# A hybrid transformer on one core: value and gate blocks taken earlier, the norms' statistics placed with priority, and each boundary's third weight block prepared ahead of the tail

## The chip, the core and the metric

The kernel runs on one core of a Trainium2 chip: TensorE multiplies matrices into PSUM, VectorE, ScalarE and GpSimd work on rows of SBUF and PSUM, and SyncE's queue carries nearly all DMAs. The metric is the device time of one execution in microseconds; times are medians of several runs, and a profile is taken from one further execution.

## The reference, cut to what matters

Two layers over 512 tokens of width 1024, each a token mixer and a feed-forward, with RMS norms before and after:

```python
for layer in range(DEPTH):
    a = rmsnorm(h, ln_mix_pre[layer])
    mem_n = rmsnorm(mem, ln_mem[layer])              # 256 memory rows
    if layer < N_A_LAYERS:                           # layer A
        proj = a @ w_in_a[layer]                     # u, v (768 each), q_mem (256)
        main = chunked_spatial_gating(u, v, ...)     # gelu(u) * (w_s @ layernorm(gelu(v)) + b_s)
    else:                                            # layer B: 12 heads with a forget gate
        main = forgetting_attention(q, k_s, v_s, log_f_s)
    mixed = concat([main, memory_attention(q_mem, mem_n, w_mem_kv[layer])])
    h = h + rmsnorm(mixed @ w_out[layer], ln_mix_post[layer])
    f = rmsnorm(h, ln_ffn_pre[layer])
    f = (silu(f @ w_ffn_gate[layer]) * (f @ w_ffn_up[layer])) @ w_ffn_down[layer]
    h = h + rmsnorm(f, ln_ffn_post[layer])
```

All of it is float32.

## The kernel before

**Products in three matmuls.** A float32 operand is kept as two parts in a format that TensorE takes at full rate: a rounded copy (`hi`) and what is left (`lo`). ScalarE makes `hi` (a cast), VectorE `lo` (a subtraction; both in `split`, L241), and `mm3` (L193 to L195) multiplies hi by hi, hi by lo and lo by hi into one PSUM tile. Weights come by DMA into one of four `raw` tiles; `weight_parts` splits each half of 512 columns into a pair `whi`, `wlo` out of eight buffers each. The activations' parts (`act`) share a pool of 36 tiles.

**What sets the order.** The program is written in the order below; a scheduler then gives each engine its own list of instructions, which the engine runs strictly in that order, each waiting for what it reads. `tc.high_priority()` lets a scheduler place the instructions inside it sooner, `issue_after` later. PSUM tiles are taken by tags: `mm` and `lg` with three buffers each, `tr` with two.

**Norms.** `Norm` sums squares of the tokens (`add`). `finish` multiplies the sum on TensorE (`st`), VectorE adds the epsilon (`var`), GpSimd raises it to the power -1/2 (`r`, L262). `spread` spreads the result over all partitions by transposes on TensorE (`rb`), and VectorE copies it out.

**The start of layer A** (`layer_a`, from L568). While h's squares are summed, TensorE works on query and value projections. `value_block(j)` makes eight pieces for one third of the value columns, each piece 12 matmuls of 256 columns; three such blocks (24 pieces, v_1 to v_12 in the lists) are one filler queue. The start takes 1, 2, 1, 1 and 3 of them between its steps: the norm of h, the loads of the memory rows, the query's scaling, the sums of the memory rows, the memory keys' weights, the memory rows' norm (`norm.finish((0, NMEM))`, var_2 and rb_2). Then come the memory keys (ps_3, ps_4), the memory values (memv) and the memory attention of four heads, between whose steps the remaining 16 pieces are put, four to a head. After the attention `gate_inputs(m)` makes one gate block (u): 24 matmuls of 512 columns and a Gelu. `stats`, `normed` and `spatial` make the layer norm of the gated values (mv, rv, vhi, vlo) and the spatial product s; gate blocks 0, 1 and 2 stand between the attention and the first s.

**The boundaries** (`boundary`). At the end of the first mixer, of the first feed-forward and of the second mixer the same function closes one stage and opens the next. `tail(0)` to `tail(3)` are the last products of the old stage for four blocks of 128 tokens, each with its own norm (ss, v, r) and scaling of y; `turn` transposes y (yt), adds it to h, and makes the next stage's inputs (hs, xshi, xslo) and squares (sq) for half of the tokens. The next stage's first four weight blocks are multiplied with the first half of tokens in `group(..., lag=3)`: three blocks go in step, the fourth lags three inputs. The first two blocks' weights were prepared behind `tail(1)`, the third's and fourth's behind the last `turn` of the first half. The norm of that half (st_3, var_3, rb_3 at the first boundary) is finished inside the group.

Of the kernel before, what the change touches and what calls it, by code (L numbers as in the profile page):

```python
# [15 lines left out]
P = 128  # L16
T = 512
D = 1024
KT = 8
TB = T // P  # L20
NMEM = 256
# [5 lines left out]
RMS_EPS = 1e-6  # L27
# [13 lines left out]
def hybrid(ctx: ExitStack, tc: tile.TileContext, i: dict, out: bass.AP):  # L41
# [91 lines left out]
    def pair_of_parts(n=512, aside=False):  # L133
        if aside:
            return act("whi"), act("wlo")
        return (wp.tile([P, max(n, 512)], F32R, tag="hi", name=name("whi"), bufs=8)[:, :n],
                wp.tile([P, max(n, 512)], F32R, tag="lo", name=name("wlo"), bufs=8)[:, :n])
# [10 lines left out]

    def prepared(src, shape, eng=None):

        raw = wp.tile([P, 1024], F32, tag="raw", name=name("raw"), bufs=4)
        n = shape[0] * shape[1]
        dst = raw[:, :n].rearrange("p (a b) -> p a b", a=src.shape[1]) if len(src.shape) == 3 else raw[:, :n]
        last_load[0] = nc.sync.dma_start(dst, src)
        return weight_parts(raw, shape, eng)

    def weight_parts(raw, shape, eng=None):
        n = shape[0] * shape[1]
        parts = []
        for d in range(0, n, 512):  # L160
            pair = pair_of_parts(min(512, n - d))
            split(raw[:, d : min(d + 512, n)], *pair, eng)
            parts += cut(pair, shape[1])
        return parts
# [99 lines left out]
    class Norm:  # L264
# [16 lines left out]
        def finish(self, cols):  # L281

            c0, c1 = cols
            tbs = range(c0 // P, c1 // P)
            t0, t1 = c0 // P, c1 // P
            st = ps("tr", (P, 4), s="st")
            for tb in tbs:
                some = self.sums(tb, cols)
                for n, sq in enumerate(some):
                    PE.matmul(st[:, tb : tb + 1], sq, avg, start=n == 0, stop=n == len(some) - 1)  # L290
            v = small("var")
            V.tensor_scalar_add(v[:, t0:t1], st[:, t0:t1], RMS_EPS)
            rsqrt(self.r4[:, t0:t1], v[:, t0:t1], t1 - t0)

# [270 lines left out]
    def layer_a():  # L565
        a = parts("a")
# [27 lines left out]
        def value_block(j):  # L594

            w, o = [], []

            def load():
                for kh in range(2):
                    w.extend(prepared(i["w_a_v"][j, kh], (4, 256)))  # L600

            def piece(tk, kh):
                if kh == 0:
                    o.append(ps("mm", (P, 256), s="v"))
                c = slice(tk * P, (tk + 1) * P)
                for k in range(4 * kh, 4 * kh + 4):
                    mm3(o[tk], (a[k][0][:, c], a[k][1][:, c]), w[k], k == 0, k == KT - 1)
                if kh:
                    evacs.append(lambda: evacuate(tk))
                if pre.done:  # L610
                    while evacs:
                        evacs.pop(0)()

            def evacuate(tk):
                if tk % 2 == 0:
                    vg[j, tk // 2] = plain("vg", (P, 2, 256))
                A.activation(vg[j, tk // 2][:, tk % 2, :], o[tk], AF.Copy, scale=pre.r4[:, tk : tk + 1])

            return load, [lambda tk=tk, kh=kh: piece(tk, kh) for tk in range(TB) for kh in range(2)]

        with tc.tile_pool(name="sgu", bufs=1) as lp:
            bsp = lp.tile([P, NG, P], F32, name="bsp")
            fill = queue([value_block(j) for j in range(3)])
            outs = [ps(t) for t in ("mm", "lg")]
# [16 lines left out]
            memt = load_mem()  # L641
            pieces(1)
            pre.spread(FULL, rbc)
# [3 lines left out]
            norm = mem_sums(memt)  # L647
            pieces(1)
            xs = mem_inputs(0, memt)
            wk = mem_key_weights(0)  # L650
            norm.finish((0, NMEM))
            pieces(3)
            norm.spread((0, NMEM), rmem)
# [7 lines left out]
            with tc.issue_after(last_exp[0].ins):  # L661
                for vt in vg.values():
                    A.activation(vt, vt, AF.Gelu_apprx_tanh)
# [3 lines left out]
                   for n, x in enumerate(("ln_v_g", "ln_v_b"))])  # L667
# [5 lines left out]
                            compare_op=ALU.is_ge, fill=0.0, base=0, channel_multiplier=-1)  # L673
            us, vp = [], {}
            mv = lp.tile([P, TB, 2], F32, name="mv")
            rv = small("rv")

            wu = []

# [43 lines left out]

            gate_inputs(0)
            stats()
# [131 lines left out]
    def boundary(phase, post, pre, nnorm, dst, block, evac, scaled=None):  # L857
# [37 lines left out]
        with behind(phase_parts):  # L895
            ws = [block(n) for n in range(2)]
        tail(2)
        turn(0, range(2))
        tail(3, lambda: turn(0, (2,)))
        turn(0, (3,))  # L900
        ws += [block(n) for n in range(2, 4)]
        outs = group(ws, inputs(0), h0, ["mm", "lg"] * 2, lag=3,
# [139 lines left out]
    def feed_forward(layer, phase, xp, meanwhile=None):  # L1042
# [32 lines left out]

        def first(n):
            return prepared(i["w_up" if n % 2 else "w_gate"][layer, n // 2], (KT, P))

# [50 lines left out]
    def layer_b(phase, fp):  # L1129
# [16 lines left out]
        def evac_first(outs, cols):  # L1146
            for m, o in zip(first, outs):
                queries(m, o, cols)

        a, close = boundary(phase, G_FFN_POST, G_MIX_PRE + 1, bnorm, rbc,  # L1150
                            lambda n: prepared(i["w_b_q"][first[n]], (KT, P)), evac_first)
        for m in range(2, 6):
# [256 lines left out]
```

## Time and profile before

| what | value |
|---|---|
| median of 3 runs | 1122.04 us (1121.86 to 1122.38) |
| the profiled execution | 1121.42 us, of which the span of its instructions 1119.7 us |
| VectorE, ScalarE busy | 80%, 59% of the span |
| DMA | 118.12 MB in all, 105 GB/s on average |

The span runs from the first to the last instruction of the profile; the rest of the execution's time lies around it. A busy share is an average over stages. Where TensorE loses time is read from the waits of its matmuls and of its weight loader (PEld), which stand in the part on the prediction. Each row of a timeline gives start, duration, engine, line, operation, what it writes and reads, shape, how often in a row, and in brackets the engine's idle time before it with what ended it.

### The profile page before, as it was taken

How to read it: one execution, taken by the hardware profiler on the slowest of the kernel's cores; microseconds unless marked ns; L12 is line 12 of the kernel's file. 1: busy time of each engine (PE TensorE's matmuls, PEld its weight loads, DVE VectorE, ACT ScalarE, POOL GpSimd, SP SyncE). 2: the span in 40 equal slices, each digit the busy share in tenths (PEclk: the TensorE clock that was granted, in tenths of full speed). 3: DMA queues.
4: the chain of work that ended last, by engine and by line, in shares of the span. 5: the costliest groups of instructions: out<-in, count | busy, mean ns of one | idle time of the engine just before them, and what ended most of it. 6: DMA issues, size and time to landing. Idle time of an engine off the chain costs nothing.

```text
span 1119.7 us, 19536 instructions
## 1 busy us (share of the span) xinstructions
PE 1107.3 (99%) x7409; PEld 1002.7 (90%) x7409; DVE 892.0 (80%) x1721; ACT 660.3 (59%) x1388; POOL 28.5 (3%) x41
## 2 busy tenths in 40 slices
PE   8999999999999999999999999999999999999998
PEld 6998889999899899998988898889999899899996
DVE  7979448999598578796968889958998598588776
ACT  7775458755266255476757677768765266255453
POOL 0100001000000000001000000001000000000000
PEclk9999999999999999999999999999999999999999
DMA  7413231334224234244242655421235234233222
GB/s 265 151 49 109 77 97 58 100 108 151 76 89 140 74 99 127 76 135 148 63 128 59 153 128 137 135 76 57 65 106 152 74 101 133 70 109 118 76 76 76
DMA packets 63557, 118.12 MB, mean 105 GB/s; under 512 B 5164, under 2 KB 39992, under 8 KB 63464
## 3 DMA queue, kind: packets, MB, share of 16 engines
q1 hardware_dynamic: 62584, 116.05, 33.8%
q8 instruction: 58, 0.95, 0.4%
q0 software_dynamic: 192, 0.52, 0.2%
q10 hardware_dynamic: 688, 0.31, 0.1%
q14 instruction: 35, 0.29, 0.1%
HBM read 104.71 MB, written 2.10 MB: 95 GB/s over the span
## 4 chain that ended last, share of the span: by engine, by line
PE 86%; DVE 7%; ACT 3%; issue 2%; POOL 1%; DMA 1%; SPq 0%; POOLq 0%; DVEq 0%; ACTq 0%
PE y L193 9%; PE y L195 9%; PE y L194 9%; PE a L194 5%; PE a L193 5%; PE a L195 5%; PE ps L195 3%; PE ps L194 3%; PE ps L193 3%; PE e L193 3%; PE e L194 3%; PE x L194 3%; PE x L193 3%; PE x L195 3%; PE e L195 3%; DVE wlo L241 2%
## 5 line engine op out<-in xcount | busy, mean ns | idle before, releaser
L241 ACT CAST whi<-raw 128x512 fp32r<-128x512 f32 x460 | 276.2, 620 | 267.0 <-PE y L195 118.6
L241 DVE TENSOR_TENSOR wlo<-raw,whi 128x512 fp32r<-128x512 f32 x460 | 305.2, 685 | 108.8 <-ACT whi L241 106.6
L193 PE MATMUL y<-whi,fhi 128*128 128x512 f32 (+1 forms) x356 | 140.0, 394 | 0.0
L194 PE MATMUL y<-wlo,fhi 128*128 128x512 f32 (+1 forms) x356 | 139.4, 392 | 0.0
L195 PE MATMUL y<-whi,flo 128*128 128x512 f32 (+1 forms) x356 | 139.4, 392 | 0.0
L194 PE MATMUL a<-xslo,whi 128*128 128x256 f32 x320 | 90.0, 281 | 0.0
L194 PE MATMUL x<-xslo,whi 128*128 128x256 f32 x320 | 89.9, 281 | 0.0
L195 PE MATMUL x<-xshi,wlo 128*128 128x256 f32 x320 | 89.9, 281 | 0.0
L193 PE MATMUL x<-xshi,whi 128*128 128x256 f32 x320 | 89.8, 281 | 0.0
L193 PE MATMUL a<-xshi,whi 128*128 128x256 f32 x320 | 89.8, 281 | 0.0
L195 PE MATMUL a<-xshi,wlo 128*128 128x256 f32 x320 | 89.8, 281 | 0.0
L193 PEld LDWEIGHTS y<-whi,fhi 128*128 128x128 f32 x356 | 66.9, 188 | 15.7 <-ACT fhi L241 0.7
L195 PEld LDWEIGHTS y<-whi,flo 128*128 128x128 f32 x356 | 66.9, 188 | 15.5 <-DVE flo L241 0.2
L194 PEld LDWEIGHTS y<-wlo,fhi 128*128 128x128 f32 x356 | 67.0, 188 | 14.7 <-DVE wlo L241 0.2
L193 PE MATMUL ps<-xshi,whi 128*128 128x256 f32 (+1 forms) x224 | 67.5, 304 | 0.0
L195 PE MATMUL ps<-xshi,wlo 128*128 128x256 f32 (+1 forms) x224 | 67.1, 302 | 0.1
L194 PE MATMUL ps<-xslo,whi 128*128 128x256 f32 (+1 forms) x224 | 66.4, 299 | 0.0
L193 PEld LDWEIGHTS a<-xshi,whi 128*128 128x128 f32 x320 | 60.4, 189 | 0.4
L194 PEld LDWEIGHTS a<-xslo,whi 128*128 128x128 f32 x320 | 60.3, 188 | 0.3
L193 PEld LDWEIGHTS x<-xshi,whi 128*128 128x128 f32 x320 | 60.4, 189 | 0.0
L195 PEld LDWEIGHTS x<-xshi,wlo 128*128 128x128 f32 x320 | 60.3, 189 | 0.0
L194 PEld LDWEIGHTS x<-xslo,whi 128*128 128x128 f32 x320 | 60.3, 188 | 0.0
(283 smaller groups left out, 3091.1 us busy)
## 6 DMA issues: line engine op xcount, KB each, us to landing
raw<-in_w_gate SPq DMA_DIRECT2D x44, 512.0 KB, 3.6
raw<-in_w_up SPq DMA_DIRECT2D x44, 512.0 KB, 3.5
raw<-in_w_down SPq DMA_DIRECT2D x44, 512.0 KB, 4.0
raw<-in_w_out SPq DMA_DIRECT2D x16, 512.0 KB, 4.5
raw<-in_w_b_q SPq DMA_DIRECT2D x8, 512.0 KB, 3.5
raw<-in_w_a_v SPq DMA_DIRECT2D x6, 512.0 KB, 7.0
raw<-in_w_a_u SPq DMA_DIRECT2D x6, 512.0 KB
raw<-in_w_v SPq DMA_DIRECT2D x6, 512.0 KB, 3.7
```

What stands on the lines that cost most here:

```text
L193: PE.matmul(o, w[0], x[0], start=start, stop=False, skip_group_check=more)
L194: PE.matmul(o, w[0], x[1], start=False, stop=False, skip_group_check=more)
L195: return PE.matmul(o, w[1], x[0], start=False, stop=stop, skip_group_check=more)
L241: last_parts[:] = A.copy(hi, src), (eng or V).tensor_sub(lo, src, hi)
```

## The change

Four edits in one diff; no instruction is added or taken away on any engine, only places and tiles change.

1. The start of layer A takes 1, 2, 2, 2 and 5 value pieces instead of 1, 2, 1, 1 and 3. So the weights of the second value block are loaded and split ahead of the memory keys', and v_5 and v_6 come ahead of the memory keys. The memory rows' `finish` is written ahead of the memory keys' weights. The third value tile takes the PSUM tag `lg`.
2. Gate block 0 becomes four pieces at the end of the filler queue. With 12 value pieces spent at the start, 12 value pieces and these four fill the attention. Its Gelu follows those of the values.
3. In `Norm.finish`, var and the power stand under `tc.high_priority()`.
4. At each boundary the third block is prepared with the first two, behind `tail(1)`, and its parts lie in four tiles of the large pool instead of the pool of weight parts. Only the fourth is left for later.

```diff
-    def prepared(src, shape, eng=None):
+    def prepared(src, shape, aside=False):
...
-            pair = pair_of_parts(min(512, n - d))
-            split(raw[:, d : min(d + 512, n)], *pair, eng)
+            pair = pair_of_parts(min(512, n - d), aside)
+            split(raw[:, d : min(d + 512, n)], *pair)
...
             v = small("var")
-            V.tensor_scalar_add(v[:, t0:t1], st[:, t0:t1], RMS_EPS)
-            rsqrt(self.r4[:, t0:t1], v[:, t0:t1], t1 - t0)
+            with tc.high_priority():
+                V.tensor_scalar_add(v[:, t0:t1], st[:, t0:t1], RMS_EPS)
+                rsqrt(self.r4[:, t0:t1], v[:, t0:t1], t1 - t0)
...
-                    o.append(ps("mm", (P, 256), s="v"))
+                    o.append(ps("lg" if (j, tk) == (0, 2) else "mm", (P, 256), s="v"))
...
-            fill = queue([value_block(j) for j in range(3)])
+            us, wu = [], []
+
+            def gate_block(m):
+
+                o = []
+
+                def load():
+                    wu.append(prepared(i["w_a_u"][m], (KT, P)))
+
+                def piece(n):
+                    if n == 0:
+                        o.append(ps("mm", s="u"))
+                    for k in range(2 * n, 2 * n + 2):
+                        mm3(o[0], wu[m][k], a[k], k == 0, k == KT - 1)
+                    if n == 3:
+                        us.append(plain("u"))
+                        V.tensor_mul(us[m], o[0], rbc)
+
+                return load, [lambda n=n: piece(n) for n in range(4)]
+
+            fill = queue([value_block(j) for j in range(3)] + [gate_block(0)])
...
             memt = load_mem()
-            pieces(1)
+            pieces(2)
             pre.spread(FULL, rbc)
...
             norm = mem_sums(memt)
-            pieces(1)
+            pieces(2)
             xs = mem_inputs(0, memt)
+            norm.finish((0, NMEM))
             wk = mem_key_weights(0)
-            norm.finish((0, NMEM))
-            pieces(3)
+            pieces(5)
             norm.spread((0, NMEM), rmem)
...
-                for vt in vg.values():
+                for vt in (*vg.values(), us[0]):
                     A.activation(vt, vt, AF.Gelu_apprx_tanh)
...
-            gate_inputs(0)
             stats()
...
         with behind(phase_parts):
-            ws = [block(n) for n in range(2)]
+            ws = [block(n, n == 2) for n in range(3)]
         tail(2)
         turn(0, range(2))
         tail(3, lambda: turn(0, (2,)))
         turn(0, (3,))
-        ws += [block(n) for n in range(2, 4)]
+        ws.append(block(3, False))
```

**TensorE around rb_2**, the broadcast of the memory rows' norm. Before (ps_3 is the first memory key block, v_1 to v_12 are value tiles):

```order
L193 MATMUL ps_3_533<-mparts_4_393,whi_9_410 128x256
L194 MATMUL ps_3_533<-mparts_4_393,whi_9_410 128x256
L195 MATMUL ps_3_533<-mparts_4_393,wlo_9_411 128x256
L259 MATMUL rb_2_496<-ident_91,r4_2_359 128x128 x2
L193 MATMUL ps_3_533<-mparts_5_396,whi_10_414 128x256
L194 MATMUL ps_3_533<-mparts_5_396,whi_10_414 128x256
L195 MATMUL ps_3_533<-mparts_5_396,wlo_10_415 128x256
```

and with the change:

```order
L193 MATMUL v_6_523<-whi_12_400,ahi_8_132 128x256
L194 MATMUL v_6_523<-wlo_12_401,ahi_8_132 128x256
L195 MATMUL v_6_523<-whi_12_400,alo_8_133 128x256
L259 MATMUL rb_2_549<-ident_91,r4_2_372 128x128 x2
L193 MATMUL ps_3_586<-mparts_1_431,whi_13_465 128x256
L194 MATMUL ps_3_586<-mparts_1_431,whi_13_465 128x256
L195 MATMUL ps_3_586<-mparts_1_431,wlo_13_466 128x256
```

The broadcast stood in the middle of ps_3, 48 matmuls behind its sums; now it stands ahead of ps_3, behind v_5 and v_6 (24 matmuls each), 60 behind its sums. rb_1, of the norm of h, stood in front of v_3 and now stands in its middle, 12 matmuls later.

**VectorE at the same place**: the memory norm's var_2, the gain products of the memory rows (mparts) and the low parts of weights. Before:

```order
L246 SCALAR_TENSOR_TENSOR mparts_8_405<-mem_4_329,gains_89,mparts_8_405 128x256
L241 TENSOR_TENSOR wlo_9_411<-raw_5_408,whi_9_410 128x512
L241 TENSOR_TENSOR wlo_10_415<-raw_5_408,whi_10_414 128x512
L241 TENSOR_TENSOR wlo_11_421<-raw_6_418,whi_11_420 128x512
L241 TENSOR_TENSOR wlo_12_425<-raw_6_418,whi_12_424 128x512
L292 TENSOR_SCALAR var_2_433<-st_2_428 128x2
L241 TENSOR_TENSOR wlo_13_439<-raw_7_436,whi_13_438 128x512
```

and with the change:

```order
L246 SCALAR_TENSOR_TENSOR mparts_1_431<-mem_1_326,gains_89,mparts_1_431 128x256
L667 SCALAR_TENSOR_TENSOR q_1_368<-ps_1_181,rbc_115 128x512
L667 SCALAR_TENSOR_TENSOR q_2_369<-ps_2_182,rbc_115 128x512
L246 SCALAR_TENSOR_TENSOR mparts_2_434<-mem_1_326,gains_89,mparts_2_434 128x256
L293 TENSOR_SCALAR var_2_460<-st_2_455 128x2
L246 SCALAR_TENSOR_TENSOR mparts_3_437<-mem_2_327,gains_89,mparts_3_437 128x256
L246 SCALAR_TENSOR_TENSOR mparts_4_440<-mem_2_327,gains_89,mparts_4_440 128x256
```

var_2 stood behind all eight gain products and four low parts; now it stands behind the second gain product. The four low parts wlo_9 to wlo_12, now of the second value block, stand ahead of rb_1's copy.

**VectorE at the first boundary**: low parts of the third block (wlo_59, wlo_60) and the fourth (wlo_61, wlo_62). Before:

```order
L241 TENSOR_TENSOR xslo_3_1990<-hs_3_1986,xshi_3_1989 128x512
L826 SCALAR_TENSOR_TENSOR h_114<-yt_4_2016,gains_89,h_114 128x256
L241 TENSOR_TENSOR wlo_59_2037<-raw_29_2034,whi_59_2036 128x512
L826 SCALAR_TENSOR_TENSOR h_114<-yt_5_2106,gains_89,h_114 128x256 x2
L320 TENSOR_TENSOR sq_17_1944<-sq_17_1944,sq_22_2030 128x512
L241 TENSOR_TENSOR xslo_4_2027<-hs_4_2023,xshi_4_2026 128x512
L322 TENSOR_TENSOR sq_17_1944<-sq_17_1944 128x256
L241 TENSOR_TENSOR wlo_60_2041<-raw_29_2034,whi_60_2040 128x512
L241 TENSOR_TENSOR wlo_61_2047<-raw_30_2044,whi_61_2046 128x512
L241 TENSOR_TENSOR wlo_62_2051<-raw_30_2044,whi_62_2050 128x512
```

and with the change:

```order
L241 TENSOR_TENSOR xslo_3_2000<-hs_3_1996,xshi_3_1999 128x512
L844 SCALAR_TENSOR_TENSOR h_114<-yt_4_2026,gains_89,h_114 128x256
L241 TENSOR_TENSOR wlo_61_2047<-raw_30_2044,whi_61_2046 128x512
L321 TENSOR_TENSOR sq_17_1954<-sq_17_1954,sq_22_2040 128x512
L241 TENSOR_TENSOR xslo_4_2037<-hs_4_2033,xshi_4_2036 128x512
L323 TENSOR_TENSOR sq_17_1954<-sq_17_1954 128x256
L241 TENSOR_TENSOR wlo_62_2051<-raw_30_2044,whi_62_2050 128x512
L844 SCALAR_TENSOR_TENSOR h_114<-yt_5_2106,gains_89,h_114 128x256 x2
L844 SCALAR_TENSOR_TENSOR h_114<-yt_6_2122,gains_89,h_114 128x256 x2
L241 TENSOR_TENSOR wlo_63_2357<-raw_31_2354,whi_63_2356 128x512
L241 TENSOR_TENSOR wlo_64_2361<-raw_31_2354,whi_64_2360 128x512
```

wlo_59 and wlo_60 are gone from here (they stand ahead of tail(2)'s first sum), wlo_61 and wlo_62 have taken their places, and wlo_63 and wlo_64, of the next stage, stand here too, ahead of var_3. On TensorE, rb_3 with the change:

```order
L290 MATMUL st_3_2210<-avg_106,sq_17_1954 128x1 x2
L195 MATMUL ps_13_2057<-xshi_4_2036,wlo_62_2051 128x256
L193 MATMUL ps_14_2248<-xshi_5_2116,whi_55_1876 128x256
L194 MATMUL ps_14_2248<-xslo_5_2117,whi_55_1876 128x256
L195 MATMUL ps_14_2248<-xshi_5_2116,wlo_55_1877 128x256
L193 MATMUL ps_15_2249<-xshi_5_2116,whi_57_1886 128x256
L194 MATMUL ps_15_2249<-xslo_5_2117,whi_57_1886 128x256
L259 MATMUL rb_3_2228<-ident_91,r4_3_1757 128x128 x2
```

Before, 23 matmuls stood between the sums st_3 and rb_3; now six.

More of the change, by code (lines that the diff above doesn't have):

```diff
@@ L154, in prepared, with weight_parts @@
         last_load[0] = nc.sync.dma_start(dst, src)
-        return weight_parts(raw, shape, eng)
-    def weight_parts(raw, shape, eng=None):
+        return weight_parts(raw, shape, aside)
+    def weight_parts(raw, shape, aside=False):
         n = shape[0] * shape[1]
@@ L673, in layer_a @@
                             compare_op=ALU.is_ge, fill=0.0, base=0, channel_multiplier=-1)
-            us, vp = [], {}
+            vp = {}
             mv = lp.tile([P, TB, 2], F32, name="mv")
             rv = small("rv")
-            wu = []
             def gate_inputs(m):
@@ L1074, in feed_forward, with first @@
         fs = [(act("fhi"), act("flo")) for _ in range(2)]
-        def first(n):
-            return prepared(i["w_up" if n % 2 else "w_gate"][layer, n // 2], (KT, P))
+        def first(n, aside):
+            return prepared(i["w_up" if n % 2 else "w_gate"][layer, n // 2], (KT, P), aside)
         def evac_first(outs, cols):
@@ L1150, in layer_b @@
         a, close = boundary(phase, G_FFN_POST, G_MIX_PRE + 1, bnorm, rbc,
-                            lambda n: prepared(i["w_b_q"][first[n]], (KT, P)), evac_first)
+                            lambda n, aside: prepared(i["w_b_q"][first[n]], (KT, P), aside), evac_first)
         for m in range(2, 6):
```

## The prediction

> **What bounds the kernel now.** I read the page first: busy shares, the granted clock, the chain that ended last.
>
> ```profile
> PE 1107.3 (99%) x7409; PEld 1002.7 (90%) x7409; DVE 892.0 (80%) x1721; ACT 660.3 (59%) x1388; POOL 28.5 (3%) x41
> ...
> PEclk9999999999999999999999999999999999999999
> ...
> PE 86%; DVE 7%; ACT 3%; issue 2%; POOL 1%; DMA 1%; SPq 0%; POOLq 0%; DVEq 0%; ACTq 0%
> ```
> TensorE is busy for 99% of the span, its clock is granted in every slice, and it carries 86% of the chain. The change adds and removes no matmul: it only puts work in another order. So it can only touch what TensorE loses between matmuls, at most the 1% idle on the page (1119.7 - 1107.3 = 12.4 us, 1.1%), and in the stretches it reorders far less. Next I read TensorE's waits in those stretches: in the first layer's start (20 to 100 us), then at the first of the three stage boundaries (160 to 193 us), where the weight loader (PEld) shows them best.
>
> ```profile
> PEld rb L259 <- POOL r L262: 2.6, 2, 1.9
> PEld mo L485 <- ACT pT L241: 0.6, 1, 0.6
> PEld tr L456 <- PE v L195: 0.5, 1, 0.5
> ...
> PEld yt L821 <- ACT y L814: 0.7, 1, 0.7
> PEld rb L259 <- POOL r L262: 0.4, 1, 0.4
> PEld ps L193 <- ACT whi L241: 0.2, 1, 0.2
> ```
>
> Columns: waiter, what ended the wait, us in total, times, longest. The first three rows are the start: 2.6 + 0.6 + 0.5 = 3.7 us, of which the two broadcasts of a norm's root (rb) lose 2.6, one 1.9 and so the other 0.7. The last three are the first boundary, 1.3 us; the third boundary (752 to 780 us) answers with the same three rows to the digit, and the second with one row of 0.3:
>
> ```profile
> PEld ps L195 <- DVE wlo L241: 0.3, 1, 0.3
> ```
>
> All of it together is about 6.6 us, 0.6% of the time. That is the ceiling of the change; 0.2% (2.2 us) is about what a measurement of this kernel can tell from no change.
>
> **The start of layer_a: rb_1 and rb_2.**
>
> ```profile
> 26.24 0.28 PE L195 MATMUL v<-whi,alo 128*128 128x256 f32 x1
> 26.99 0.65 PE L259 MATMUL rb<-ident,r 128*128 128x128 f32 x4 [0.47 <-POOL r L262]
> ...
> 35.44 0.28 PE L195 MATMUL ps<-mparts,wlo 128*128 128x256 f32 x1
> ...
> 37.44 0.43 PE L259 MATMUL rb<-ident,r 128*128 128x128 f32 x2 [1.73 <-POOL r L262]
> ...
> 25.29 0.16 DVE L292 TENSOR_SCALAR var<-st 128x4 f32<-128x4 f32 x1 [1.57 <-PE st L290]
> ...
> 31.86 2.49 DVE L241 TENSOR_TENSOR wlo<-raw,whi 128x512 fp32r<-128x512 f32 x4
> 34.27 0.15 DVE L292 TENSOR_SCALAR var<-st 128x2 f32<-128x2 f32 x1
> 34.34 2.48 DVE L241 TENSOR_TENSOR wlo<-raw,whi 128x512 fp32r<-128x512 f32 x4
> ...
> 25.53 1.41 POOL L262 TENSOR_TENSOR r<-var,mhalf 128x4 f32<-128x4 f32 x1 [22.60 <-DVE var L292]
> 34.49 2.89 POOL L262 TENSOR_TENSOR r<-var,mhalf 128x2 f32<-128x2 f32 x1 [7.56 <-DVE var L292]
> ```
>
> Matmuls of 256 columns start about 0.118 us apart, so after 26.24 the next could start at 26.36, and rb_1 starts at 26.99: 0.63 lost. Likewise 37.44 - 35.56 = 1.88 at rb_2. Both wait for GpSimd's power.
>
> rb_1 gets 12 value matmuls put ahead of it (12 x 0.118 = 1.41), so it is due at 27.77. The power ended at 25.53 + 1.41 = 26.94; then nothing is lost. But behind its var VectorE's next work is no longer gain products but the low parts of the value weights now loaded first (wlo_9 to wlo_11), and beside four such low parts the power took 2.89: it would end at 28.42, 0.65 late. I take 0.2 lost, nearer to the 1.41 row, whose neighbours were also VectorE operations: 0.7 - 0.2 = **0.5 saved** (0 to 0.7).
>
> rb_2: its sums (st_2) now stand 60 matmuls ahead of it instead of 48, because v_5 and v_6 come before the memory keys, and its var stands at once behind mparts_2 instead of behind four low parts (2.49). Walking VectorE's new order with rb_1 at 28.0 (an estimate): rbc copied by about 30, two query products of 0.6 and two gain products of 0.4 by 32.5, var by 33. TensorE reaches rb_2 at about 28.0 + 0.4 + 84 x 0.118 = 38.3. Between them are 5.3 us, against 2.89 for the slowest power: no wait, **1.9 saved** (1.6 to 1.9).
>
> **A rule beside the 2.89.** That power started 0.15 us behind the first of four low parts that ran end to end to 36.82, and ended 0.57 after the last; alone it takes about as much as that 0.57:
>
> ```profile
> 160.84 0.56 POOL L262 TENSOR_TENSOR r<-v,mhalf 128x1 f32<-128x1 f32 x1 [4.98 <-DVE v L795]
> ```
>
> The Trainium skill, "SBUF — State Buffer", section "SBUF: two separate sides", says that VectorE and GpSimd share a pair of ports under an exclusive lock, taken by a VectorE operation with two SBUF inputs, and that "the other fully blocks". By that rule the power behind var_2 would have to sit out six gain products and four low parts, to about 38.0 + 0.56, and rb_2 would wait 0.3 instead of nothing. The power at 34.49 agrees; the one at 25.53, with three two-input operations behind its var, ended after 1.41, so the trace does not show it as strict. What a slow power would do at the other broadcasts is a rival below, priced from the rows.
>
> **The first transpose of the memory attention** (tr): four value pieces have moved from inside the attention to its front, and the softmax whose end it waits for still has 24 value matmuls between its last logits and the transpose; on VectorE, though, one of the value weights' low parts stands among its steps instead of three, so its products end 2 x 0.6 = 1.2 us earlier against the logits. I take its 0.5 as gone (0 to 0.5). The memory values (memv) come close instead: by the same walk their last low part is ready 0.4 us before its matmul. I book 0.1 lost (0 to 1.5, the delay of one slow power). The wait at mo (0.6) stays.
>
> **What pays for it: the gate block moved into the attention.** Before, three gate blocks stood between attention and the first spatial product; now two do.
>
> ```profile
> 89.10 0.15 DVE L694 TENSOR_SCALAR rv<-mv 128x4 f32<-128x4 f32 x1
> ...
> 94.45 0.68 DVE L241 TENSOR_TENSOR vlo<-vg,vhi 128x512 fp32r<-128x512 f32 x1
> ...
> 89.40 1.31 POOL L262 TENSOR_TENSOR rv<-rv,mhalf 128x4 f32<-128x4 f32 x1 [42.75 <-DVE rv L694]
> ...
> 97.16 0.40 PE L194 MATMUL ps<-alo,whi 128*128 128x512 f32 x1
> ...
> 98.56 0.40 PE L194 MATMUL ps<-alo,whi 128*128 128x512 f32 x1
> ...
> 100.90 0.27 PE L195 MATMUL s<-whi,vlo 128*128 128x128 f32 x1
> ```
>
> The second low part of the normed values is ready at 95.13, the first product that uses low parts starts at 100.90: 5.8 us of slack. A gate block is 24 matmuls of 512 columns, (98.56 - 97.16) / 6 = 0.233 apart: 5.6 us of that slack go. The chain gets shorter by what gate 0 had put in it on VectorE (two low parts and one product, 3 x 0.6 = 1.8) and longer by a seventh Gelu (0.6), so about 1.3 us of slack is left (an estimate). A power of 2.89 instead of 1.31 would use that up and 0.3 more. I book **0.1 lost** (0 to 1.6).
>
> Start together: -0.5 - 1.9 - 0.5 + 0.1 + 0.1 = **-2.7** (-3.1 with every lower price; +1.5 with every upper one).
>
> **The boundaries.** The third block's parts are cast and subtracted ahead of the last two token blocks' tail, while ScalarE and VectorE wait for TensorE there. So its 0.2 and the yt wait of 0.7 go, with some starts of 0.1 behind them: 12 matmuls of the third and 12 of the fourth block now stand ahead of the yt that waited. The yt groups shrink from five to two:
>
> ```profile
> 188.22 0.43 PE L259 MATMUL rb<-ident,r 128*128 128x128 f32 x2 [0.18 <-POOL r L262]
> 188.41 0.36 PE L195 MATMUL ps<-xshi,wlo 128*128 128x256 f32 x1
> 188.62 0.28 PE L193 MATMUL ps<-xshi,whi 128*128 128x256 f32 x1
> ```
>
> Behind a transpose the next step is 0.21 instead of 0.118; three groups fewer give about 0.2. But the fourth block now takes the third one's late places:
>
> ```profile
> 178.09 0.69 DVE L320 TENSOR_TENSOR sq<-sq,sq 128x512 f32<-128x512 f32 x1 [0.46 <-ACT sq L317]
> 178.70 0.69 DVE L241 TENSOR_TENSOR xslo<-hs,xshi 128x512 fp32r<-128x512 f32 x1
> 179.30 0.42 DVE L322 TENSOR_TENSOR sq<-sq 128x256 f32<-128x256 f32 x1
> 179.63 1.89 DVE L241 TENSOR_TENSOR wlo<-raw,whi 128x512 fp32r<-128x512 f32 x3
> ...
> 186.86 0.15 DVE L292 TENSOR_SCALAR var<-st 128x2 f32<-128x2 f32 x1
> ...
> 187.18 0.98 POOL L262 TENSOR_TENSOR r<-var,mhalf 128x2 f32<-128x2 f32 x1 [11.82 <-DVE var L292]
> ```
>
> wlo_62 stands behind the first three of these, the first of which waits for ScalarE's square of h as before; so it is done at 179.63 + 0.68 = 180.3. TensorE's first matmul here starts near 171.7; 48 of them at 0.118, eight transposes at 0.11 (with the 0.09 behind them) and eleven more matmuls later, at 179.6, it wants wlo_62: **0.7 lost**. From 180.3 on come thirteen matmuls, eight transposes and twenty-three matmuls (1.5 + 1.0 + 2.7): the sums st_3 at 185.5. rb_3 now stands six matmuls behind its sums instead of twenty-three (the fences on the change), so it is wanted at 186.4. Its var is behind two more low parts (wlo_63, wlo_64) but ahead of the last residual: by my walk at about 186.1; var to rb took 188.22 - 186.86 = 1.36; rb at about 187.5, so **1.1 lost** where 0.4 was. Two transposes and seven matmuls on (0.3 + 0.8) it stands at 188.6 where the kernel before stood at 188.62, the last row quoted for rb: **0.0** (-1.3 if wlo_62 is in time and rb_3 waits 0.5 as before; +1.9 if its power takes 2.89 instead of 0.98). The third boundary has the same rows and the same order: **0.0**. The second has four query blocks and 0.3 to save, and its var has less beside it: **-0.3** (-0.5 to 0.2).
>
> **Sum.** -2.7 + 0.0 + 0.0 - 0.3 = **-3.0 us**. The profiled execution took 1121.42 (span 1119.7), so 1118.4 in its frame; the median of the runs shown, 1122.04, is 0.6 above it, so I predict **1119.0**.
>
> **Rivals.** One more row bears on them, the power behind the second boundary, beside two low parts:
>
> ```profile
> 555.54 1.08 POOL L262 TENSOR_TENSOR r<-var,mhalf 128x2 f32<-128x2 f32 x1 [5.38 <-DVE var L292]
> ```
>
> - *The boundaries give all they hold.* If var_3 runs as soon as its sums are there and wlo_62 is in time, each saves 1.3: -2.7 - 2.6 - 0.3 = -5.6, **1116.4**. For it: the priority on var; against it: VectorE's order, in which wlo_62 stays behind a square it must wait for. 0.15.
> - *The cover was needed.* rb_1's 0.6, 0.5 at memv and 1.0 at the first spatial product eat the gain: -3.0 + 0.4 + 0.4 + 0.9 = -1.3, **1120.7**. For it: TensorE's slack there falls from 5.8 to about 1.3 us on my walk; against: each has slack, if little. 0.22.
> - *Slower: the power beside VectorE's stream.* If each power that now has low parts or sums behind its var takes 2.89, as at 34.49: 0.45 more at rb_1, 0.2 at the spatial product and 1.9 at each of the three boundaries. -3.0 + 6.35 = +3.35, **1125.4**. The place that decides is rb_3 and its two sisters: with everything else as forecast, the kernel is slower by 0.2% once their power passes 0.98 + (2.2 + 3.0) / 3 = 2.7 us. Against it: behind var_3 comes first a residual product out of PSUM, and beside two low parts the power took only the 1.08 of the row above. 0.06.
> - *It does nothing*: the waits reappear one step later, **1122.0**. The order shows the moved rows, so 0.05.
>
> **How the numbers follow.** The forecast has 0.52; most of its own spread (1118 to 1120.5) is under 1119.8, which is 0.2% below 1122.04; I give 0.44 of it to faster. Faster: 0.44 + 0.15 + 0.03 of the second = 0.62. Same: 0.08 + 0.19 + 0.05 = 0.32. Slower: 0.06. The range reaches from the first rival to just past the second, 1116.4 to 1121.4, and leaves out the slow power and part of no effect.
>
> **What would show it.** In the changed profile: rb at about 28 with under 0.3 of idle, rb at about 38 with none; memv (about 46) and the first spatial product (about 98) without a wait above 0.3; at 170 to 190 no wait at yt, but one at ps for wlo (0.7) and one at rb of about 1.0. It would be wrong if the rb waits at the boundaries pass 1.5 each, or if the spatial product waits over a microsecond.

## The result and the profile after

The changed kernel took **1114.91 us** (median of 5 runs, 1114.41 to 1117.99), the kernel before beside it 1121.88: 6.97 us less, a ratio of 0.9942 [0.9929, 0.9956]. The forecast was 1119.0 with a range of 1116.4 to 1121.4, so the sign was right, and the gain was more than twice the one forecast and outside the range. The profiled execution took 1114.41 (span 1112.7). The page's row of busy times:

```profile
PE 1103.1 (99%) x7409; PEld 1000.2 (90%) x7409; DVE 891.2 (80%) x1721; ACT 660.5 (59%) x1388; POOL 25.4 (2%) x41
```

TensorE's idle time went from 12.4 to 9.6 us (1112.7 - 1103.1): 2.8 us, close to the 3.0 forecast. But its *busy* time fell too, by 4.2 us (1107.3 - 1103.1), with the same 7409 matmuls. No step of the prediction had that. (The split is rough: the profile counts part of a short wait as busy, as at rb_1 before, where 0.63 us were lost and 0.47 show as idle.)

To find both I cut TensorE's list of matmuls at the same ones in every trace and took the time from start to start. All differences are to the first execution of the kernel before; the columns are explained with the experiments below. A "spot" is a short place inside a feed-forward that moves from execution to execution.

| stretch (us of the trace before) | before | before, again | changed | changed, again | start only | aside only | four aside | sums' own bank |
|---|---|---|---|---|---|---|---|---|
| first 100 matmuls, 1.3 to 24.3 | 23.04 | +0.52 | -0.55 | +0.22 | -0.03 | +0.58 | -0.13 | +0.32 |
| layer A, to 132.3 | 108.00 | -0.01 | **-3.51** | -3.48 | -3.47 | -0.01 | -3.53 | -3.52 |
| first boundary, to 211.3 | 79.00 | +0.01 | **-0.03** | -0.04 | -0.03 | -0.24 | +0.04 | -0.85 |
| second boundary, 516.8 to 564.5 | 47.66 | -0.01 | +0.02 | +0.03 | +0.15 | +0.03 | +0.01 | -0.35 |
| third boundary, 745.7 to 789.7 | 44.00 | -0.01 | +0.05 | +0.08 | +0.04 | +0.28 | +0.11 | -0.28 |
| first feed-forward, without 263 to 278 | 290.46 | 0.00 | **-1.28** | -1.27 | -1.01 | -0.45 | -0.77 | -1.04 |
| layer B, 564.5 to 745.7 | 181.18 | +0.01 | +0.01 | -0.02 | +0.07 | +0.07 | -0.11 | -0.01 |
| second feed-forward, without 851 to 865 | 251.54 | +0.05 | **-0.91** | -0.90 | -0.03 | -1.15 | +0.11 | -0.95 |
| end, from 1055.3 | 60.18 | +0.03 | -0.17 | -0.15 | +0.02 | -0.17 | +0.02 | -0.17 |
| spot at 263.4 to 278.5 | 15.09 | +1.02 | -0.77 | -0.15 | +0.15 | +0.19 | -0.70 | +0.18 |
| spot at 850.7 to 864.8 | 14.09 | +0.49 | -0.04 | +0.19 | +0.80 | -0.17 | -0.13 | +0.92 |

The -7.17 us of the first pair are: layer A -3.5, the boundaries nothing, the steady stretches of the feed-forward layers and the end -2.35, and the start's first matmuls and the two spots -1.35.

**The start.** These are TensorE's waits in the changed kernel as the weight loader shows them: the first two rows from 20 to 100 us, the next three from 155 to 190 (and the same three, to the digit, from 745 to 775), the last from 520 to 550.

```profile
PEld mo L486 <- ACT pT L241: 0.5, 1, 0.5
PEld vcols L749 <- PE ps L194: 0.4, 1, 0.4
...
PEld ps L195 <- DVE wlo L241: 0.8, 1, 0.8
PEld rb L259 <- POOL r L262: 0.5, 1, 0.5
PEld st L290 <- issue: 0.3, 1, 0.3
...
PEld st L290 <- issue: 0.3, 1, 0.3
```

The two waits at rb and the one at tr are gone from the start. The timeline around the two broadcasts and the first spatial product (start, duration, engine, line, operation, and the wait in front of it, if any):

```profile
27.11 0.28 PE L195 MATMUL v<-whi,alo 128*128 128x256 f32 x1
27.23 0.60 PE L259 MATMUL rb<-ident,r 128*128 128x128 f32 x4
...
38.33 0.28 PE L195 MATMUL v<-whi,alo 128*128 128x256 f32 x1
38.45 0.38 PE L259 MATMUL rb<-ident,r 128*128 128x128 f32 x2
...
96.88 0.27 PE L195 MATMUL s<-whi,vlo 128*128 128x128 f32 x1
...
24.98 1.41 POOL L262 TENSOR_TENSOR r<-var,mhalf 128x4 f32<-128x4 f32 x1 [22.05 <-DVE var L293]
31.71 0.90 POOL L262 TENSOR_TENSOR r<-var,mhalf 128x2 f32<-128x2 f32 x1 [5.32 <-DVE var L293]
...
25.42 1.89 DVE L241 TENSOR_TENSOR wlo<-raw,whi 128x512 fp32r<-128x512 f32 x3
...
31.56 2.46 DVE L246 SCALAR_TENSOR_TENSOR mparts<-mem,gains,mparts 128x256 fp32r<-128x256 f32 x6
...
95.14 0.68 DVE L241 TENSOR_TENSOR vlo<-vg,vhi 128x512 fp32r<-128x512 f32 x1
```

Each rb starts 0.12 behind the matmul ahead of it, one matmul's pace: no time is lost. rb_1's power was done at 24.98 + 1.41 = 26.39, 0.8 ahead of its broadcast, beside the three low parts that start at 25.42; rb_2's was done at 32.61, 5.8 ahead. The normed values' second low part was ready at 95.82 and wanted at 96.88: 1.06 us of slack, where 1.3 was worked out.

**The first boundary.** The same view at the places where the prediction walked:

```profile
175.54 0.69 DVE L241 TENSOR_TENSOR wlo<-raw,whi 128x512 fp32r<-128x512 f32 x1
...
181.17 0.87 DVE L844 SCALAR_TENSOR_TENSOR h<-yt,gains,h 128x256 f32<-128x256 f32 x2
182.41 0.16 DVE L293 TENSOR_SCALAR var<-st 128x2 f32<-128x2 f32 x1 [0.37 <-PE st L290]
...
181.38 0.27 PE L194 MATMUL ps<-xslo,whi 128*128 128x256 f32 x1
181.80 0.58 PE L290 MATMUL st<-avg,sq 128*128 128x1 f32 x4
...
182.91 0.28 PE L194 MATMUL ps<-xslo,whi 128*128 128x256 f32 x1
183.50 0.43 PE L259 MATMUL rb<-ident,r 128*128 128x128 f32 x2 [0.31 <-POOL r L262]
...
182.74 0.70 POOL L262 TENSOR_TENSOR r<-var,mhalf 128x2 f32<-128x2 f32 x1 [11.47 <-ACT sq L318]
```

This execution stands 0.55 + 3.51 = 4.06 ahead of the one before here. Put back by that, wlo_62 was done at 180.29 (forecast 180.3) and rb_3 stood at 187.56 (forecast 187.5). The new waits were 0.8 for wlo_62 (0.7 was priced), 0.3 in front of the sums and 0.5 in front of the broadcast (1.1 was priced, all of it at the broadcast), and they took the place of the old ones. var ran 0.37 us behind VectorE's work before it, as soon as its sums were there. The two low parts that stand ahead of it in VectorE's list, wlo_63 and wlo_64, had run long before and held nothing up:

```profile
177.71 1.28 DVE L241 TENSOR_TENSOR wlo<-raw,whi 128x512 fp32r<-128x512 f32 x2
```

### The profile page after: what moved, and what is told of

It is laid out like the page before. It is cut to its first block, busy times and chain, and to the rows that moved or that the text cites. A ratio compares the mean times of both kernels' runs of the same rounds, so it can differ in the third digit from the quotient of the medians.

```text
span 1112.7 us, 19537 instructions
## 1 busy us (share of the span) xinstructions
PE 1103.1 (99%) x7409; PEld 1000.2 (90%) x7409; DVE 891.2 (80%) x1721; ACT 660.5 (59%) x1388; POOL 25.4 (2%) x41
## 4 chain that ended last, share of the span: by engine, by line
PE 89%; DVE 5%; ACT 3%; issue 1%; DMA 1%; POOL 0%; SPq 0%; POOLq 0%; DVEq 0%; ACTq 0%
PE y L193 9%; PE y L195 9%; PE y L194 9%; PE a L195 5%; PE a L193 5%; PE a L194 5%; PE e L193 3%; PE e L195 3%; PE x L193 3%; PE x L195 3%; PE e L194 3%; PE x L194 3%; PE ps L195 3%; PE ps L193 3%; PE ps L194 3%; PE v L193 2%
```

## The experiments

**What varies by itself, and what belongs to the program.** Both kernels were run once more, unchanged. First the kernel before:

> The kernel before, unchanged, as a control. The two traces differ by 7.0 us of span: about 3.5 us lie at the start of layer A, 0.8 in one product at 266 us, 0.6 in the first hundred matmuls, which are the same in both, and some 2.2 us are spread thinly over stretches in which the order is the same (23.70 us for 200 matmuls of 256 columns before, 23.52 with the change). Theory 1, the thin part belongs to the execution: this run's 200 matmuls take anything from 23.5 to 23.7 and its time differs from the shared runs of before by up to 2 us. Theory 2, it belongs to the program: 23.70 again, within 0.03, and a ratio of 1.000 within 0.0005.

It took 1121.88 beside 1121.44, ratio 1.0004 [0.9995, 1.0012]. Its profiled execution was the longest of the set, 2.1 us above the first trace of before, and the table says where: in the first 100 matmuls and the two spots; all other stretches agree within 0.05. At the first spot ScalarE's casts wait for a weight that arrives by DMA. Before:

```profile
269.95 0.62 ACT L241 CAST whi<-raw 128x512 fp32r<-128x512 f32 x1 [1.32 <-DMA raw<-in_w_down]
```

and before, again, in the timeline and in TensorE's waits from 262 to 276:

```profile
271.94 1.14 ACT L241 CAST whi<-raw 128x512 fp32r<-128x512 f32 x2 [2.89 <-DMA raw<-in_w_down]
```

```profile
PE y L193 <- DVE s L1009: 0.8, 1, 0.8
PE e L193 <- ACT s L1003: 0.3, 1, 0.3
```

The cast waited 1.6 longer for the same load, and what stands behind it on ScalarE and VectorE made TensorE wait 0.8 where before it didn't. So this place is luck of an execution. The first 100 matmuls and the second spot also move between two executions of one program, by 0.2 to 0.8 us; what moves them was not followed up. The long stretch, by contrast, repeats. In the timelines of the kernel before, its first and last matmul are

```profile
278.47 0.39 PE L193 MATMUL y<-whi,fhi 128*128 128x512 f32 x1
...
516.85 0.39 PE L193 MATMUL y<-whi,fhi 128*128 128x512 f32 x1
```

and in its second execution

```profile
280.00 0.39 PE L193 MATMUL y<-whi,fhi 128*128 128x512 f32 x1
...
518.38 0.39 PE L193 MATMUL y<-whi,fhi 128*128 128x512 f32 x1
```

238.38 us both times for 1650 matmuls. In the changed kernel:

```profile
273.45 0.39 PE L193 MATMUL y<-whi,fhi 128*128 128x512 f32 x1
...
510.70 0.39 PE L193 MATMUL y<-whi,fhi 128*128 128x512 f32 x1
```

237.25. The busy times by stretch (columns: window, its length, then busy time and count of PE, PEld, DVE, ACT and POOL, the granted clock, the DMA share and GB/s) say that it is not a wait. Before, then changed:

```profile
278.50:516.80 238.30, 238.30 (x1651) 221.49 (x1650) 187.32 (x320) 121.82 (x242) 2.27 (x4) 1.00 0.35 107
```

```profile
273.40:510.70 237.30, 237.30 (x1651) 220.44 (x1651) 186.34 (x319) 121.61 (x242) 2.27 (x4) 1.00 0.36 107
```

TensorE is busy in every instant of both, with as many matmuls, at a granted clock of 1.00. Busy alone does not rule out short waits, since a matmul of 512 columns is booked for 0.39 us and the next starts 0.23 behind it. The gaps from start to start do: none of the 1650 is over 133 ns (256 columns) or 241 ns (512 columns) before, or over 125 and 244 ns in the changed kernel. So no single wait makes the difference; it is the same work at another pace. The changed kernel once more:

> The changed kernel, unchanged, as the other half of the control. Theory 1 (the thin part belongs to the execution): 200 matmuls anywhere from 23.5 to 23.7, ratio 0.994 to 0.997. Theory 2 (it belongs to the program): 23.52 within 0.03 and 0.9940 to 0.9945.

1116.08, ratio 0.9953 [0.9941, 0.9965]; its long stretches stand within 0.03 of the first changed execution's (237.26 for the one above); its spots do not. Without the three places the change is worth 7.17 - 1.35 = 5.8 us in the traces, and the medians of the two sets, 6.97 and 5.36, lie on both sides of that.

**Which part gives what.** The start alone, without the priority and with the boundaries as before:

```diff
-            with tc.high_priority():
-                V.tensor_scalar_add(v[:, t0:t1], st[:, t0:t1], RMS_EPS)
-                rsqrt(self.r4[:, t0:t1], v[:, t0:t1], t1 - t0)
+            V.tensor_scalar_add(v[:, t0:t1], st[:, t0:t1], RMS_EPS)
+            rsqrt(self.r4[:, t0:t1], v[:, t0:t1], t1 - t0)
...
-            ws = [block(n, n == 2) for n in range(3)]
+            ws = [block(n, False) for n in range(2)]
...
-        ws.append(block(3, False))
+        ws += [block(n, False) for n in range(2, 4)]
```

> The start of layer A and the moved gate block alone; no priority on the statistics, third block as before. If the start is worth what the trace shows there (3.5 us) and nothing else follows from it: 1118.3 to 1118.6, ratio 0.9970. If the thin part hangs on this half of the change: about 1116. Without the priority var_2 may stand behind the gain products again, and rb_2 wait up to 1 us: then 1119.5.

1118.09, 0.9972 [0.9962, 0.9983]. Layer A gives its 3.47 without the priority. And the first feed-forward gives 1.01, though from layer A's end on the lists of all five engines are those of the kernel before, instruction by instruction: only the tiles lie elsewhere, since layer A took them in another order.

The other half, the third block's parts in the large pool and nothing else:

```diff
-            ws = [block(n) for n in range(2)]
+            ws = [block(n, n == 2) for n in range(3)]
...
-        ws += [block(n) for n in range(2, 4)]
+        ws.append(block(3, False))
```

> The third block's parts prepared ahead of the tail, alone; start and statistics as before. Forecast theory (the removed waits return at the fourth block and at rb): 1121.5 to 1122.1. If rb keeps its late place because there is no priority: up to 1.3 us less at each of two boundaries, 1119.3. If the thin part or the product at 266 us hangs on this half: another 0.8 to 3 us less.

1119.99, 0.9985 [0.9977, 0.9994]. The three boundaries together give +0.06, nothing. What it gains is in the steady stretches: -0.45 and -1.15. Neither half has the priority on the statistics. The start saves as much without it as with it, and the first boundary came out at -0.24 without it and -0.03 with it, so no gain from the priority shows anywhere; it was not tried alone.

The start without its gate block, which stands behind the attention again:

```diff
-            fill = queue([value_block(j) for j in range(3)] + [gate_block(0)])
+            fill = queue([value_block(j) for j in range(3)])
...
-                for vt in (*vg.values(), us[0]):
+                for vt in vg.values():
...
+            gate_inputs(0)
             stats()
```

> The value pieces taken earlier and the memory norm's earlier place, without the gate block in the attention: the last head of the memory attention then has no filler between its steps. If the gate block is what pays for the earlier pieces, the waits of that head come out: a head has four pieces of 1.4 us, and its softmax chain is about as long, so 2 to 5 us back, 1120 to 1123. If it is not needed, the same 3.5 us are saved as with it (about 1118.1).

1118.42, 0.9972 [0.9961, 0.9983]. Layer A still gives 3.13. So the gate block is no cover that the rest needs; it is worth 0.34, and the waits from 20 to 100 us say by what:

```profile
PEld mo L485 <- ACT pT L241: 0.7, 2, 0.4
PEld vcols L749 <- PE ps L194: 0.4, 1, 0.4
PEld tr L456 <- issue: 0.3, 1, 0.3
```

Without it the attention runs out of filler, and 0.5 more stands at mo and tr.

The fourth block prepared aside as well:

```diff
-            ws = [block(n, n == 2) for n in range(3)]
+            ws = [block(n, n >= 2) for n in range(4)]
...
-        ws.append(block(3, False))
```

> The changed kernel with the fourth block too prepared behind tail(1) in the large pool. The wait for wlo_62 (0.8 us at each of the first and third boundary) goes; if rb then comes due earlier by the same 0.8 while its var stays behind VectorE's residuals, its wait grows by as much and nothing is gained (ratio to the changed kernel 1.000, about 1116); if the four casts and subtractions were what held var back, 0.7 to 1.0 each are gained (about 1114.3).

1116.77, 0.9956 [0.9944, 0.9969]: no better than the change. Its waits at the first boundary:

```profile
PEld st L290 <- issue: 1.1, 1, 1.1
PEld rb L259 <- POOL r L262: 0.5, 1, 0.5
```

The 0.8 for wlo_62 is gone and stands in front of the sums, at st, instead. Something other than weights holds the sums back, and the view only calls it "issue".

**What changes the pace.** There are five edits of the kernel *before* that leave its products alone and move tiles or the list, with one execution each. The first puts 256 bytes ahead of all constants, so that every address moves; it also changed the order of TensorE's first 200 matmuls, and layer A came out 0.42 shorter. The second adds one more of the matmuls on zeros at the start, so that TensorE's list moves by one. The third takes one more pair of weight parts at the start, unused, so that the later weight parts lie elsewhere; the fourth and the fifth do the same with a PSUM tile and with a tile of the large pool:

```diff
+    pad = cp.tile([P, 64], F32, name="pad")
+    nc.vector.memset(pad, 0.0)
```

> The kernel before with one unused tile of 256 bytes per partition ahead of all others (and one VectorE memset to write it), so every SBUF address moves by 256 bytes and TensorE's list is the same. If the thin part of the gain, a steady pace that differs by up to 0.2 us in 200 equal matmuls, hangs on where operands lie, the stretches of the feed-forwards that repeat to 0.01 us between two profiles of one kernel move by more than 0.05 us here. If it hangs on TensorE's list of instructions or its neighbours, they repeat to 0.01.

```diff
-    idle(10, zero)
+    idle(11, zero)
```

> The kernel before with one more of the ten idle matmuls at its start: every later TensorE instruction stands one place further on in its list, addresses are the same. If the pace hangs on the place of instructions in the list, the feed-forward stretches move by more than 0.05 us; if on addresses, they repeat to 0.01 us. The idle matmul itself lies in the time in which the first weights are on their way, so it costs nothing.

```diff
+    for t in pair_of_parts():
+        V.memset(t.bitcast(F32), 0.0)
```

> The kernel before with one pair of weight tiles taken and set to zero at the start, so that every later weight part lies one buffer further on in its ring of eight; every engine's list is otherwise the same. If the thin part hangs on which buffer a weight part lies in, the feed-forward stretches move by 0.3 to 1.3 us in sum against the kernel before; if not, they repeat to 0.05.

```diff
+    PE.matmul(ps("mm", s="skip"), zero[:, :P], zero, start=True, stop=True)
```

> The kernel before with one PSUM tile of the tag mm taken and written by one idle matmul at the start, so that about half of the later products go to another PSUM bank; lists otherwise the same. If the thin part hangs on the banks, the feed-forward stretches move by 0.3 to 1.3 us in sum; if not, they repeat to 0.05.

```diff
+    V.memset(act("skip").bitcast(F32), 0.0)
```

> The kernel before with one tile of the large pool taken and set to zero at the start: some 600 of the 5700 later matmuls read their operands from another place. If the thin part hangs on the place of the activations' parts, the feed-forward stretches move by some tenths of a us; if not, they repeat to 0.05.

They took 1121.84, 1122.80, 1120.23, 1120.73 and 1121.17. The totals hold the luck of the three places; the stretch of 1650 matmuls doesn't. Four times it repeats the 238.38 of before. With the weight parts moved it took 515.42 - 277.76 = 237.66, again with TensorE busy throughout at a clock of 1.00:

```profile
277.76 0.40 PE L196 MATMUL y<-whi,fhi 128*128 128x512 f32 x1
...
515.42 0.40 PE L196 MATMUL y<-whi,fhi 128*128 128x512 f32 x1
```

```profile
277.70:515.40 237.70, 237.70 (x1651) 220.91 (x1651) 187.15 (x320) 121.80 (x242) 2.27 (x4) 1.00 0.35 107
```

The first feed-forward as a whole came out at -0.99 and the second at +0.08. So the pace hangs on where the weight parts lie.

The addresses that the built programs give to the tiles say what each edit moved in this stretch. With the weight parts moved, 1638 of the 1650 matmuls read their weights from another address; TensorE's list with its semaphore waits, all activations and all PSUM banks are those of before. It was no step of one buffer: buffers are handed out as they come free, and the parts are spread over their eight buffers in another order, with the whole area 16384 bytes lower. Which of the two counts was not separated. The PSUM edit moved 873 of the products to another bank and the large-pool edit 345 of the activations' reads, and the pace stayed. The gaps say the same: with the weights in place all but a few of the 1650 repeat within 2 ns (all but 32 in the second execution of before), and with the weights moved 879 change by 3 ns or more, up and down.

In the changed kernel the third block's parts lie in the large pool, and the start takes the weight parts in another order, so nearly all weights in the stretch lie elsewhere; but so do most activations, and half of the products go to another PSUM bank. That its -2.35 come from the weights fits the two half changes, but is argued from them. Why one placement is quicker than another stays open. Each buffer has a pace of its own: before, matmuls of 512 columns with weights at 224 modulo 256 bytes start 228.3 ns apart on average, and those at 128 modulo 256, 234.2. But these means alone do not add up to the differences between programs, and the shift by 256 bytes, which did nothing to this stretch, leaves them as they are.

**What holds the sums.** The sums st share the PSUM tag tr, of two buffers, with the transposed token blocks yt. In the changed kernel with st of the first half of a boundary in the tag lg:

```diff
-        def finish(self, cols):
+        def finish(self, cols, tag="tr"):
...
-            st = ps("tr", (P, 4), s="st")
+            st = ps(tag, (P, 4), s="st")
...
-                            6: lambda: nnorm.finish(h0)})
+                            6: lambda: nnorm.finish(h0, "lg")})
```

> The changed kernel with the sums st of a boundary's first half in a PSUM tile of the tag lg instead of tr, which the transposed y (yt) also use. In the changed kernel the removed waits came back as a wait at st (0.3) and at rb (0.5). If st waits for VectorE to empty a tr tile (the residuals), the wait at st goes, var and the power come earlier, and 0.3 to 0.7 us are gained at each of the three boundaries: ratio to the changed kernel 0.9985 (about 1114.5 beside 1116.1). If the sum of squares itself is late, nothing changes.

1113.84, 0.9934 [0.9921, 0.9948]. Against the changed kernel the boundaries give 0.82, 0.37 and 0.33. One row is left of the first boundary's waits,

```profile
PEld ps L195 <- DVE wlo L241: 0.8, 1, 0.8
```

and the sums follow their neighbour in one step, the broadcast in little more:

```profile
180.95 0.28 PE L195 MATMUL ps<-xshi,wlo 128*128 128x256 f32 x1
181.07 0.50 PE L290 MATMUL st<-avg,sq 128*128 128x1 f32 x4
...
182.81 0.28 PE L195 MATMUL ps<-xshi,wlo 128*128 128x256 f32 x1
182.98 0.43 PE L259 MATMUL rb<-ident,r 128*128 128x128 f32 x2
```

So st had waited for a tile that VectorE's residuals (181.17 in the changed kernel) had still to empty: of the two in that row, the first is the last reader of such a tile; by the length of a single one, 0.48, it ended at about 181.65, and the sums started at 181.80. This is the fastest of the kernels by its traced boundaries, 1.5 us ahead of the change; the intervals of the two ratios overlap, so the totals alone don't tell them apart.

## Why the prediction was right, and where it was not

- **The ceiling was the step that failed**: "So it can only touch what TensorE loses between matmuls". Of the 5.8 us that belong to the change, 2.35 are matmuls that run back to back in both kernels and run quicker in one. I took 0.118 us a matmul as fixed, from rows of one trace, and it is not. The placement of the weights alone moved 1650 of them from 238.38 to 237.66, and the change moves the weights too; that this is where its 2.35 come from is argued, not shown.
- **The start was mis-sized**: -2.7 forecast, -3.5 measured. The three waits went as described (0.7, 1.9 and 0.5, together 3.1, and the start without the gate block gives 3.13). The 0.2 at rb_1, 0.1 at memv and 0.1 at the spatial product that I booked against them didn't come: rb_1's power took 1.41, not towards 2.89, and the slack in front of the spatial product shrank about as walked, from 5.8 to 1.06 us (1.3 was expected). The gate block, booked as what pays for the rest, itself gave 0.34.
- **The boundaries were right at the first and third, in part by luck**: 0.0 forecast, -0.03 and +0.05 measured, with wlo_62 0.8 late (0.7 forecast). Of the 1.1 put down to rb, 0.3 was st waiting for its PSUM tile and 0.5 the chain from st to rb. The walk had the two low parts hold var back; in the run those had long ended and var waited for its sums, at 181.80 + 4.06 = 185.86 in the time of before (185.5 forecast). The two accounts happen to put rb_3 at the same instant. At the second I expected -0.3 and got +0.02: the wait for wlo there was replaced by st's, a limit of which the prediction had no term.
- **The spots** added 1.35 us of luck to the first pair. Without them the 5.8 would give 1122.0 - 5.8 = 1116.2, still just under the range.
- **The rivals.** The slow power didn't come: 0.90 at rb_2, 0.70 at the first boundary. That the boundaries give all they hold would have been -2.9 at the three; with st in another tag they give 1.5. That the cover was needed did not come either: rb_1 and memv had no wait, and the first spatial product had 1.06 of slack. None of the rivals had the steady stretches move.

## What to carry to other kernels

A TensorE that is busy for 99% of the span is not yet at a fixed pace: here the same back-to-back matmuls took 238.4 or 237.7 us by where their weights lay. So an edit that changes which buffers are taken can move the time by a tenth of a percent or so without any wait, and an edit that moves the weight tiles and nothing else is the cheap test of it. Before explaining a difference, cut both traces at the same matmuls, and take a second execution of each kernel: stretches that repeat to 0.05 us belong to the program, those that move by 1 us to the execution. A wait that the view calls "issue" in front of a matmul is worth a try with the output in another PSUM tag.

## What the runs showed of the hardware

- The addresses of the weight parts change the matmuls' pace: 238.38 against 237.66 us for 1650 of them, which is 0.4 ns for each, with no idle time and at the same granted clock. Two executions of one program agree in such a stretch within 0.05 us.
- GpSimd's power on a 128x2 tile took 0.90 us beside the six gain products of 31.56 and 0.70 beside one residual product, where it had taken 2.89 beside four low parts. The prediction read the lock of the Trainium skill, "SBUF — State Buffer", section "SBUF: two separate sides", as held through a whole run of two-input operations, so that the first of these powers would have had to sit out the products and the four low parts behind them. The section of the Trainium skill has the pair of ports held "for the whole instruction". Here the power ended at 32.61, inside the run of gain products from 31.56 to 34.02, and the wait of 0.3 at rb_2 that I derived from the strict reading did not come. A lock held for one instruction at a time would allow that; the 2.89 beside four low parts shows that GpSimd does not always get in between.
